# Hybrid attention, scan and MLP block on one core: a ring for keys and values, and other margins in the order planner

## The chip, the cores and the metric

The kernel runs on one core of a Trainium2 chip. The metric is the device time of one execution in microseconds, as the median of several runs. The program text runs once on the host and writes a fixed list of instructions for each engine: TensorE (PE), VectorE (DVE), ScalarE (ACT), GpSimd (POOL) and SyncE (SP), which issues all DMAs. Each engine works through its own list in order and waits on semaphores.

## The reference

One layer over 2048 tokens of width 1024, all in float32 (shortened):

```
h = rmsnorm(x); q, k, v, z, xbc, dt, qx = split(h @ w_in)
q, k = partial_rope(rmsnorm per head)                      # 8 query heads, 2 key/value heads, 64 wide
attn_out = windowed_gqa(q, k, v, sink)                     # each 128-token block sees blocks j-1, j, j+1
ssd_out  = bidirectional_ssd(z, xbc, dt, ...)              # 16 heads, chunks of 128 tokens, both directions
xatt_out = memory_cross_attention(qx, mem, ...)            # 256 memory tokens
x = x + concatenate([attn_out, ssd_out, xatt_out]) @ w_out
x = x + square(relu(rmsnorm(x) @ w_mlp_up)) @ w_mlp_down   # hidden width 4096
```

In the windowed attention a query at position p sees keys with |p - p'| <= 128, so of block j-1 the upper triangle, of block j everything, of block j+1 the lower triangle; the softmax has one more column, the sink.

## The kernel before

A large product is made of two-part operands (hi + lo, rounded to the fp32r format) in three matmuls. There are three stages.

Stage 1 (`stage1`, line 1095) goes over the tokens in two halves, the second half first. For each it loads x transposed, splits it (`split`, line 466: ScalarE writes hi, another engine lo), and makes keys and values, the convolution columns, cross attention, and queries. `kvdt_tiles` (line 887) stores for each block of 128 tokens the transposed keys to `k_d` in DRAM (four rows of 128 tokens: hi and lo of two heads), laid out as 128 partitions x 4 x 2048 tokens, and the values to `v_d`.

Stage 2 (`stage2`, line 1331) goes over the 16 blocks j and the two key/value heads: 32 times an attention unit (`att_unit`, line 1201) and a scan unit (`ssd_unit`, line 1264), and 24 times a column block of the gate z (`z_col`, 24 full-width matmuls of 512 columns). `att_load` (line 1190) loads for each unit its queries, its window of two or three key blocks (tile `kw`, two buffers) and of value blocks (`vw`, two buffers). The unit makes the scores of four heads, adds a mask of three blocks (line 524: triangle, zeros, other triangle), takes exp, transposes, and multiplies with the values. This last product, and the scan's product per head, have stationary operands of 64 columns and write one half of the partitions; two of them run side by side.

Stage 3 (`stage3`, line 1618) makes the output projection for 8 pairs of token tiles (`out_pair`, line 1370; the weights w_out come through two raw buffers, `raw` in line 605, and `out_weights` splits them), then the MLP in a seven-product scheme (`seven`, line 1520), whose moving blocks come from `xc_d` and whose sums are added to rows of x1, loaded at the stage's start.

The order on all engines is written out by a planner. Every operation is first recorded with a cost and its dependences (`add`, line 197). `plan` (line 277) then runs a model of the engines: each time an engine is free it takes, of the operations whose inputs are ready, the one earliest in the program among those that are safe, otherwise the one that becomes safe first. Safe is ready plus a margin (`margin`, line 269), which depends on the engine of the producer o and of the consumer q. For a DMA the model counts 475 ns on SP, then

```
dma = max(dma, s + 1100) + o.bytes / 360.0
o.end = dma + 900
```

A switch between 64-column and full-width matmuls counts 95 ns. `schedule` (line 389) then issues the operations in the order of their planned starts, and the engines keep to it whatever the real times are.

SBUF is cut into regions with names (`memory1` to `memory4`), each reused by a later stage once everything that touched it is done; inside a region a tag has a number of buffers that are used in turn.

Of the kernel before, what the change touches and what calls it, by code (L numbers as in the profile page):

```python
# [10 lines left out]
F32 = mybir.dt.float32  # L11
F32R = mybir.dt.float32r
I32 = mybir.dt.int32
AF = mybir.ActivationFunctionType
# [5 lines left out]
P = 128  # L20
D = 1024
T = 2048
NJ = T // P
# [7 lines left out]
EPS = 1e-6  # L31
# [4 lines left out]
NCOL, NROW = sum(n for _, n in COLS), sum(n for _, n in ROWS)  # L36
# [37 lines left out]
class Program:  # L74
# [193 lines left out]
    @staticmethod  # L268
    def margin(o, q):

        if o.eng == "SP":
            return 2500
        if q.eng == "PE" and o.eng != "PE":
            return 800
        return 0 if o.eng == q.eng or o.eng == "PE" else 200

    def plan(self):

# [172 lines left out]
class Hybrid:  # L451
# [53 lines left out]
    def constants(self):  # L505
        nc, a = self.nc, self.a
        sizes = dict(ident=128, ones=128, eps=1, cols=NCOL, r1=16)
        self.mem.use("const", F32, **{"c_" + k: (n, 1) for k, n in sizes.items()})
        sizes = dict(triU=128, triL=128, amask=384, rows=NROW, dt=512, acs=512, wst=512, dec=512, edge=48, negA=32)
        self.mem.use("late", F32, **{"c_" + k: (n, 1) for k, n in sizes.items()})  # L510

        def c(name, shape):
            return self.mem.tile([P] + shape, F32, "c_" + name)

        self.ident = c("ident", [P])
        make_identity(nc, self.ident)
        self.ones = c("ones", [P])
        nc.gpsimd.memset(self.ones, 1.0)
        self.triU = c("triU", [P])
        self.triL = c("triL", [P])  # L520
        for t, sgn in ((self.triU, 1), (self.triL, -1)):
            nc.gpsimd.affine_select(out=t, in_=self.ones, compare_op=ALU.is_ge, fill=0.0, base=0,
                                    pattern=[[sgn, P]], channel_multiplier=-sgn)
        self.mask = c("amask", [3 * P])
        nc.gpsimd.memset(self.mask, 0.0)
        for o, sgn in ((0, 1), (2 * P, -1)):
            m = self.mask[:, o:o + P]
            nc.gpsimd.affine_select(out=m, in_=m, compare_op=ALU.is_ge, fill=NEG, base=0,
                                    pattern=[[sgn, P]], channel_multiplier=-sgn)
        self.eps = c("eps", [1])  # L530
        nc.gpsimd.memset(self.eps, EPS)

        cols, rows = c("cols", [NCOL]), c("rows", [NROW])
        first = NCOL - 256
        self.load(cols[:, :first], a["cols"][:, :first])

        def cut(t, table, name, shape=None):
            at = sum(n for k, n in table[:[k for k, _ in table].index(name)])
            v = t[:, at:at + dict(table)[name]]
            return v.rearrange("p (a b) -> p a b", a=shape[0]) if shape else v  # L540

        self.w_mix, self.w_mem, self.w_mlp, self.w_ssd, self.cb, self.sd = (
            cut(cols, COLS, n) for n in ("w_mix", "w_mem", "w_mlp", "w_ssd", "cb", "sd"))
        self.cw, self.cos, self.sin = cut(cols, COLS, "cw", (NXC,)), cut(cols, COLS, "cos", (NJ,)), cut(cols, COLS, "sin", (NJ,))
        for v in (cut(cols, COLS, "cw"), self.cb):
            nc.vector.tensor_scalar(v, v, 0.5, None, ALU.mult)
        self.qw, self.kw, self.xqw, self.xkw, self.sink, self.dtb, self.al = (
            cut(rows, ROWS, n) for n in ("qw", "kw", "xqw", "xkw", "sink", "dtb", "al"))
        self.r1 = c("r1", [NJ])
        self.dt = c("dt", [NJ, 32])  # L550
        self.acs = c("acs", [NJ, 32])
        self.wst = c("wst", [NJ, 32])
        self.dec = c("dec", [NJ, 32])
        self.edge = c("edge", [NXC, 4])
        self.negA = c("negA", [32])
        yield
        self.load(cols[:, first:], a["cols"][:, first:])
        self.load(rows, a["rows"].rearrange("(o n) -> o n", o=1).broadcast_to([P, NROW]))
        nc.vector.tensor_scalar(self.qw, self.qw, 0.125, None, ALU.mult)
        nc.vector.tensor_tensor(self.xkw, self.xkw, self.xqw, ALU.mult)  # L560
        nc.scalar.activation(self.negA, self.al, AF.Exp)
        nc.vector.tensor_scalar(self.negA, self.negA, -1.0, None, ALU.mult)
        yield
# [20 lines left out]
    def memory2(self):  # L584
        m = self.mem
        m.use("E", F32R, mv=(1024, 2), qs=(512, 2))
        m.use("A1", F32R, sr=(1024, 2), kw=(768, 2), vw=(192, 2, F32))
        m.use("A0", F32, fr=(1024, 2), xw=(512, 2), ao=(256, 2))
        m.use("B", F32, xs=(1280, 2), sf0=(512, 2), sf1=(512, 2), xb=(1536, 2))
        m.use("C", F32, ap=(1536, 2))  # L590
        m.use("X0", F32R, zxh=(512, 8))
        m.use("X1", F32R, zxl=(512, 8))
        m.use("X2", F32, apT=(1536, 2), y=(512, 2))
        m.use("X3", F32R, zwh=(1024, 2), zwl=(1024, 2))
        m.use("W0", F32, bk=(1024, 2), pb=(1024, 2))
        m.use("W1", F32, ee=(1024, 2), zth=(512, 2))
        m.use("Z", F32, zwr=(1024, 1), zraw=(512, 2), zrow=(512, 1), zt=(512, 2))

    def memory3(self):
        m = self.mem  # L600
        for i, (h, l) in enumerate((("X0", "X1"), ("late", "A1"), ("X2", "A0"), ("W0", "W1"))):
            m.use(h, F32R, **{f"woh{i}": (1024, 4)})
            m.use(l, F32R, **{f"wol{i}": (1024, 4)})
        m.use("X3", F32R, ah=(512, 4), al=(512, 4))
        m.use("Z", F32, raw=(1024, 2), ar=(512, 2))
        m.use("B", F32, row=(1024, 4), xn=(1024, 2), yr=(512, 4))
        m.use("C", F32, mb=(512, 6))
        m.use("E", F32R, ms=(1024, 2), zg=(512, 2))
# [17 lines left out]
    def scratch(self):  # L626
        dp = self.ctx.enter_context(self.tc.tile_pool(name="dram", bufs=1, space=DRAM))
        d = lambda name, shape, dt=F32: dp.tile(shape, dt, name=name, tag=name)
        self.r_d = d("r_d", [T])
        self.xbc_d = d("xbc_d", [NJ, P, NXC, P])  # L630
        self.xst_d = d("xst_d", [NJ, P, XST_W])
        self.v_d = d("v_d", [NJ, P, P])
        self.k_d = d("k_d", [P, 4, T])
        self.q_d = d("q_d", [NJ, P, 8 * P])
        self.row_d = d("row_d", [NJ, 2, 2, 2, 2, 8, 64])
        self.srow_d = d("srow_d", [NJ, 2, 2, 8, 3, P])
        self.erow_d = d("erow_d", [NJ, 2, 2, 8, P])
        self.pb_d = d("pb_d", [NJ, P, D])
        self.z_d = d("z_d", [NJ, P, 8, P])
        self.mix_d = d("mix_d", [NJ, P, 16, P])  # L640
        self.x1_d = d("x1_d", [T, D])
        self.xc_d = d("xc_d", [2, 8, 2, 4, P, BLK])
# [244 lines left out]
    def kvdt_tiles(self, pool, t0, tts, ps):  # L887

        nc = self.nc
# [7 lines left out]
        kk = pool.tile([P, BLK], F32, "tm")  # L897
        self.head_norm(pool, [ps[tt][:, 0:P] for tt in tts], 2, 64, r, self.kw, kk, "tm")
        for i in range(4):
            j = j0 + i  # L900
# [11 lines left out]
                nc.tensor.transpose(pt[:, n * P:(n + 1) * P], ktv[:, n, :], self.ident)  # L912
            ko = pool.tile([P, 4, P], F32R, "ko")
            nc.scalar.copy(ko, pt.rearrange("p (i t) -> p i t", i=4))
            self.store(self.k_d[:, :, j * P:(j + 1) * P], ko.bitcast(F32))

    def dt_half(self, pool, t0):

# [269 lines left out]
        self.store(self.z_d[b * 4:b * 4 + 4, :, c, :].rearrange("j p t -> p j t"), zt.rearrange("p (j t) -> p j t", j=4))  # L1188

    def att_load(self, pool, j, kv):  # L1190
        lo, hi = max(j - 1, 0), min(j + 1, NJ - 1)
        n = hi - lo + 1
        qs = pool.tile([P, 4, P], F32R, "qs")
        self.load(qs.bitcast(F32).rearrange("p h t -> p (h t)"), self.q_d[j][:, kv * BLK:(kv + 1) * BLK])
        kk = pool.tile([P, 2, 3 * P], F32R, "kw")
        self.load(kk[:, :, :n * P].bitcast(F32), self.k_d[:, kv * 2:kv * 2 + 2, lo * P:(hi + 1) * P])
        vv = pool.tile([P, 3, 64], F32, "vw")
        self.load(vv[:, :n, :], self.v_d[lo:hi + 1, :, kv * 64:kv * 64 + 64].rearrange("j t c -> t j c"))
        return n, lo - j + 1, qs, kk, vv

    def att_unit(self, pool, j, kv):
        nc = self.nc
        n, m0, qs, kk, vv = self.att_load(pool, j, kv)
        w = n * P
# [6 lines left out]
        mask = self.mask[:, m0 * P:m0 * P + w]  # L1211
        for i in range(4):
            ps = self.ps()[:, :w]
            nc.tensor.matmul(ps, qs[:, i, :], kk[:, 0, :w], start=True, stop=False)
            nc.tensor.matmul(ps, qs[:, i, :], kk[:, 1, :w], start=False, stop=True)
            nc.vector.tensor_tensor_reduce(pr[:, i, :], ps, mask, 1.0, NEG, ALU.add, ALU.max, mx[:, i:i + 1])
        nc.vector.tensor_tensor(mx, mx, sk, ALU.max)
        nc.vector.tensor_scalar(ng, mx, -1.0, None, ALU.mult)
# [112 lines left out]
    def stage2(self):  # L1331
# [4 lines left out]
        for n, (ts, ring) in enumerate(((self.mv, "fr"), (self.sr, "fr"))):  # L1336
            raw = pool.tile([P, 1024], F32, ring)
            self.load(raw, self.a["pick"][n])
            for t in ts:
                nc.scalar.copy(t, raw)  # L1340
        self.sf = []
        for g in range(2):
            st = pool.tile([P, BLK], F32, f"sf{g}")
# [387 lines left out]
```

## Time and profile before

| | us |
|---|---|
| median of 3 runs | 2802.86 (2800.09 to 2805.92) |
| the profiled execution | 2797.64 |
| its span, first to last instruction | 2795.8 |
| PE busy | 2743.8 (98%) |
| DVE, ACT, POOL busy | 1887.1, 1361.1, 554.1 |
| share of the DMA queue in 16 engines' span | 55.5% |

PE, the matrix engine, is busy nearly all the time. Busy time of PE includes the time of matmuls in the pipeline, so idle time alone doesn't show everything. The granted clock of PE is given as a share of full speed (1.00 is 2.4 GHz).

### The profile page before, as it was taken

To read this page: it belongs to the slowest core of one execution; us is meant where nothing else is said; L and a number is where in the kernel's file an instruction comes from. 1 tells how busy PE (TensorE), PEld (TensorE's weight loads), DVE (VectorE), ACT (ScalarE), POOL (GpSimd) and SP (SyncE) were. 2 spreads that over 40 slices of the span, in tenths; PEclk is the share of its full clock that TensorE was granted. 3 is DMA by queue.
4 is the path that set the end of the run, shared out by engine and by line. 5 is a ranking of instruction groups with operands and counts; after the bars stand their busy time and mean duration, and the time that the engine had idled before them with its cause. 6 is when DMAs were issued, how large, how long until landed. Compare 5 with 4: busy or idle time off the path is not lost.

```text
span 2795.8 us, 37466 instructions
## 1 busy us (share of the span) xinstructions
PE 2743.8 (98%) x13628; PEld 2253.9 (81%) x13628; DVE 1887.1 (67%) x3133; ACT 1361.1 (49%) x2294; POOL 554.1 (20%) x488
## 2 busy tenths in 40 slices
PE   8999999999999999999999999999999999999999
PEld 8878887788777777778888788888888888888887
DVE  5884568856666686666666776675758485757666
ACT  5645543354567676843333453535344353535352
POOL 3303444445344454411010000000000000000000
PEclk9999999999999999999999999999999999999999
DMA  6661345544878787765555862627173744536251
GB/s 217 188 205 54 117 142 178 184 143 171 280 248 254 227 270 237 212 226 201 188 196 188 329 231 95 226 69 253 55 234 128 269 145 136 181 99 210 90 166 61
DMA packets 286429, 510.29 MB, mean 183 GB/s; under 512 B 36386, under 2 KB 125090, under 8 KB 286244
## 3 DMA queue, kind: packets, MB, share of 16 engines
q1 hardware_dynamic: 286244, 507.89, 55.5%
q8 instruction: 108, 1.77, 0.3%
q14 instruction: 77, 0.63, 0.1%
HBM read 390.36 MB, written 117.45 MB: 182 GB/s over the span
## 4 chain that ended last, share of the span: by engine, by line
PE 76%; DMA 4%; DVE 1%; ACT 1%; issue 1%; POOL 1%; SPq 0%; DVEq 0%; POOLq 0%; ACTq 0%
PE bank L404 76%; DMA Z<-in_xT_dram 1%; DMA W<-erow_d 1%; DMA Z<-mix_d 0%; DMA X<-xc_d 0%; ACT C L404 0%; DMA E<-z_d 0%; DMA A<-k_d 0%; DMA xst_d<-B 0%; ACT X L404 0%; DMA B<-mix_d 0%; DMA B<-x_d 0%; DVE X L404 0%; DVE Z L404 0%; DMA Z<-in_w_z_dram 0%
## 5 line engine op out<-in xcount | busy, mean ns | idle before, releaser
L404 PE MATMUL bank<-X,late 128*128 128x512 f32 x1792 | 553.7, 390 | 5.4 <-DMA X<-xc_d 5.4
L404 PE MATMUL bank<-A,E 128*128 128x512 f32 (+2 forms) x1152 | 405.2, 380 | 0.0
L404 PEld LDWEIGHTS bank<-X,late 128*128 128x128 f32 x1792 | 336.9, 188 | 75.8 <-issue 5.8
L404 PE MATMUL bank<-X,A 128*128 128x512 f32 (+1 forms) x1264 | 397.0, 390 | 0.0
L404 PE MATMUL bank<-W,X 128*128 128x512 f32 (+1 forms) x1536 | 341.5, 374 | 9.1 <-ACT W L404 7.3
L404 PE MATMUL bank<-late,E 128*128 128x512 f32 x896 | 348.5, 389 | 0.0
L404 PE MATMUL bank<-late,C 128*128 128x512 f32 x896 | 348.5, 389 | 0.0
L404 PE MATMUL bank<-X,X 128*128 128x512 f32 x1216 | 327.3, 406 | 3.0 <-ACT X L404 2.3
L404 PE MATMUL bank<-X,W 128*128 128x512 f32 x1344 | 325.1, 397 | 3.4 <-ACT W L404 3.4
L404 PEld LDWEIGHTS bank<-W,X 128*128 128x128 f32 x1536 | 268.0, 191 | 54.0 <-ACT W L404 7.3
L404 PEld LDWEIGHTS bank<-X,W 128*128 128x128 f32 x1344 | 249.1, 189 | 56.2 <-ACT W L404 3.6
L404 PEld LDWEIGHTS bank<-X,X 128*128 128x128 f32 x1216 | 225.7, 189 | 60.3 <-issue 10.6
L404 PEld LDWEIGHTS bank<-A,E 128*128 128x128 f32 x1152 | 211.6, 188 | 44.4 <-issue 6.4
L404 PEld LDWEIGHTS bank<-X,A 128*128 128x128 f32 (+1 forms) x1264 | 192.3, 173 | 51.5 <-ACT X L404 5.3
L404 DVE TENSOR_TENSOR A<-Z,late 128x1024 fp32r<-128x1024 f32 x100 | 122.1, 1222 | 138.5 <-ACT late L404 136.6
L404 DVE TENSOR_TENSOR B<-B,bank 128x512 f32<-128x512 f32 x286 | 189.7, 682 | 31.6 <-PE bank L404 31.3
L404 PEld LDWEIGHTS bank<-late,C 128*128 128x128 f32 x896 | 168.2, 188 | 35.0
L404 PEld LDWEIGHTS bank<-late,E 128*128 128x128 f32 x896 | 168.2, 188 | 34.9
L404 ACT CAST late<-Z 128x1024 fp32r<-128x1024 f32 x100 | 105.1, 1051 | 141.5 <-PE bank L404 102.1
L404 ACT ACTIVATE C<-C,small 128x384 f32<-128x384 f32 (+1 forms) x256 | 144.2, 602 | 51.9 <-DVE small L404 51.7
L404 ACT ACTIVATE W<-W 128x512 f32<-128x512 f32 x224 | 133.7, 627 | 61.5 <-DVE W L404 59.2
L404 ACT CAST E<-W 128x1024 fp32r<-128x1024 f32 x64 | 67.3, 1051 | 164.5 <-PE bank L404 164.5
(176 smaller groups left out, 4418.0 us busy)
## 6 DMA issues: line engine op xcount, KB each, us to landing
X<-xc_d SPq DMA_DIRECT2D x112, 1024.0 KB
xc_d<-E SPq DMA_DIRECT2D x56, 512.0 KB
Z<-in_w_z_dram SPq DMA_DIRECT2D x32, 512.0 KB
W<-erow_d SPq DMA_DIRECT2D x64, 256.0 KB
X<-in_w_up_dram SPq DMA_DIRECT2D x32, 512.0 KB
A<-in_w_up_dram SPq DMA_DIRECT2D x32, 512.0 KB
X<-in_w_down_dram SPq DMA_DIRECT2D x32, 512.0 KB
A<-in_w_down_dram SPq DMA_DIRECT2D x32, 512.0 KB
```

What stands on the lines that cost most here:

```text
L404: o.fn(*[fix(x) for x in o.args], **{k: fix(x) for k, x in o.kw.items()})
```

## The change

All edits go together. (1) `margin`: a 64-column matmul (`q.half`) is safe 9000 ns after its inputs are ready, a DMA that waits for compute 6000 ns (before 200, and 0 behind PE), a matmul behind another engine 1200 (800), other pairs of engines 400 (200). A consumer of a DMA keeps 2500. (2) The keys are stored block by block, and each block of keys and values, for both heads, is loaded once, at the first unit of a chunk, into place b mod 3 of a ring of three; the mask tile has six blocks, and each unit reads three (or two) of them from an offset that fits the ring's turn. (3) `eps`, which nothing reads, is set on VectorE and copied in place by ScalarE as the first instructions, instead of on GpSimd. (4) `raw` of stage 3 has three buffers.

```diff
@@ margin
         if o.eng == "SP":
             return 2500
+        if q.eng == "PE" and q.half:
+            return 9000
+        if q.eng == "SP":
+            return 6000
         if q.eng == "PE" and o.eng != "PE":
-            return 800
-        return 0 if o.eng == q.eng or o.eng == "PE" else 200
+            return 1200
+        return 0 if o.eng == q.eng or o.eng == "PE" else 400
@@ constants
+        self.eps = c("eps", [1])
+        nc.vector.memset(self.eps, EPS)
+        nc.scalar.activation(self.eps, self.eps, AF.Copy)
         self.ident = c("ident", [P])
...
-        self.mask = c("amask", [3 * P])
+        self.mask = c("amask", [6 * P])
         nc.gpsimd.memset(self.mask, 0.0)
-        for o, sgn in ((0, 1), (2 * P, -1)):
-            m = self.mask[:, o:o + P]
+        for o, sgn in ((0, 1), (2, -1), (3, 1), (5, 1)):
+            m = self.mask[:, o * P:(o + 1) * P]
...
-        self.eps = c("eps", [1])
-        nc.gpsimd.memset(self.eps, EPS)
@@ memory2, memory3, scratch, kvdt_tiles
-        m.use("A1", F32R, sr=(1024, 2), kw=(768, 2), vw=(192, 2, F32))
+        m.use("A1", F32R, sr=(1024, 2), kr=(1536, 1), vr=(384, 1, F32))
-        m.use("Z", F32, raw=(1024, 2), ar=(512, 2))
+        m.use("Z", F32, raw=(1024, 3), ar=(512, 2))
-        self.k_d = d("k_d", [P, 4, T])
+        self.k_d = d("k_d", [NJ, P, 4, P])
-            self.store(self.k_d[:, :, j * P:(j + 1) * P], ko.bitcast(F32))
+            self.store(self.k_d[j], ko.bitcast(F32))
@@ att_load
-        lo, hi = max(j - 1, 0), min(j + 1, NJ - 1)
-        n = hi - lo + 1
+        if kv == 0:
+            for b in range(j and j + 1, j + 2):
+                self.load(self.kr[:, b % 3].bitcast(F32), self.k_d[min(b, NJ - 1)])
+                self.load(self.vr[:, b % 3], self.v_d[min(b, NJ - 1)])
         qs = pool.tile([P, 4, P], F32R, "qs")
         self.load(qs.bitcast(F32).rearrange("p h t -> p (h t)"), self.q_d[j][:, kv * BLK:(kv + 1) * BLK])
-        kk = pool.tile([P, 2, 3 * P], F32R, "kw")
-        self.load(kk[:, :, :n * P].bitcast(F32), self.k_d[:, kv * 2:kv * 2 + 2, lo * P:(hi + 1) * P])
-        vv = pool.tile([P, 3, 64], F32, "vw")
-        self.load(vv[:, :n, :], self.v_d[lo:hi + 1, :, kv * 64:kv * 64 + 64].rearrange("j t c -> t j c"))
-        return n, lo - j + 1, qs, kk, vv
+        at, n = (1, 2) if j == NJ - 1 else (0, 3 if j else 2)
+        role = 4 if j == NJ - 1 else (1, 0, 2)[j % 3]
+        k = lambda l: self.kr[:, at:at + n, kv * 2 + l, :]
+        return n, role, qs, (k(0), k(1)), self.vr[:, at:at + n, kv * 64:kv * 64 + 64]
```

In `att_unit` the score matmuls read `kk[0]` and `kk[1]` instead of `kk[:, 0, :w]` and `kk[:, 1, :w]`, and `stage2` makes the two ring tiles `kr` and `vr` once.

## Rows read from the trace of the kernel before

**Rows 1.** The page: busy time of the engines, share of the span, instructions
```profile
PE 2743.8 (98%) x13628; PEld 2253.9 (81%) x13628; DVE 1887.1 (67%) x3133; ACT 1361.1 (49%) x2294; POOL 554.1 (20%) x488
```

**Rows 2.** Busy time by stage: window, PE, PEld, DVE, ACT, POOL (instructions), PEclk, DMA, GB/s
```profile
0.00:750.00 750.00, 727.47 (x3838) 609.38 (x3838) 508.43 (x1010) 370.01 (x673) 292.45 (x254) 0.99 0.52 167
750.00:1190.00 440.00, 426.52 (x2700) 328.64 (x2702) 306.75 (x760) 313.44 (x726) 209.68 (x169) 0.98 0.80 245
1190.00:1230.00 40.00, 33.22 (x146) 25.29 (x141) 24.78 (x40) 15.78 (x21) 11.06 (x13) 0.91 0.76 258
...
1585.00:1625.00 40.00, 34.57 (x146) 28.18 (x145) 18.52 (x22) 17.65 (x26) 0.00 (x0) 0.91 1.02 381
1625.00:2795.80 1170.80, 1166.97 (x5149) 965.96 (x5147) 787.41 (x821) 515.62 (x655) 0.00 (x0) 1.00 0.46 152
```

**Rows 3.** PE's timeline where it idled longest: start, us, what, [idle before <- what ended it]
```profile
353.32 1.22 PE L404 MATMUL bank<-X,W 128*128 128x512 f32 x2 [3.37 <-ACT W L404]
...
753.31 0.48 PE L404 MATMUL bank<-const,C 128*128 128x128 f32 x1 [4.42 <-ACT C L404]
...
1205.32 0.79 PE L404 MATMUL bank<-const,E 128*128 128x1 f32 x4 [2.18 <-POOL E L404]
...
1217.73 0.38 PE L404 MATMUL bank<-const,E 128*128 128x1 f32 x2 [1.40 <-POOL E L404]
...
1604.20 1.19 PE L404 MATMUL bank<-X,late 128*128 128x512 f32 x2 [5.43 <-DMA X<-xc_d]
```

**Rows 4.** Busy time by stage again, two short stretches after the last of these stops
```profile
1604.20:1607.54 3.34, 3.34 (x8) 2.69 (x9) 0.00 (x0) 0.00 (x0) 0.00 (x0) 0.50 1.05 408
1607.60:1610.94 3.34, 3.34 (x16) 2.71 (x16) 0.00 (x0) 0.00 (x0) 0.00 (x0) 1.00 1.05 415
```

**Rows 5.** Timeline of the first 8 us, ScalarE and PE
```profile
4.94 1.28 ACT L404 ACT_TABLE_LOAD   x1 [4.94 <-DMA B<-in_xT_dram]
6.23 0.72 ACT L404 ACTIVATE X<-B,const 128x512 fp32r<-128x512 f32 x1
...
7.33 0.61 PE L404 MATMUL bank<-W,X 128*128 128x288 f32 x1 [7.33 <-ACT W L404]
```

**Rows 6.** PE's timeline around 64-column matmuls (128*64): the first, one, and the last stretch
```profile
739.93 1.09 PE L404 MATMUL bank<-A,B 128*64 128x128 f32 x16
...
922.71 2.46 PE L404 MATMUL bank<-X,X 128*128 128x512 f32 x10
925.10 1.09 PE L404 MATMUL bank<-A,B 128*64 128x128 f32 x16
...
1190.50 1.04 PE L404 MATMUL bank<-A,B 128*64 128x128 f32 x16
```

**Rows 7.** PE's timeline, two short stops in stage 1
```profile
114.57 0.44 PE L404 MATMUL bank<-const,B 128*128 128x128 f32 x2 [0.70 <-ACT B L404]
...
528.03 1.55 PE L404 MATMUL bank<-B,E 128*128 128x512 f32 x3 [0.44 <-POOL B L404]
```

**Rows 8.** SP's timeline at the border to the MLP: DMA issues, count
```profile
1575.11 0.37 SPq L404 DMA_DIRECT2D X<-xc_d  x1
...
1583.96 3.37 SPq L404 DMA_DIRECT2D B<-x_d  x6
...
1588.06 1.26 SPq L404 DMA_DIRECT2D B<-x_d  x2
...
1591.39 6.85 SPq L404 DMA_DIRECT2D X<-xc_d  x3
```

**Rows 9.** DMA issues of key and value blocks: count, KB each
```profile
A<-k_d SPq DMA_DIRECT2D x28, 384.0 KB
...
A<-v_d SPq DMA_DIRECT2D x28, 96.0 KB
```

**Rows 10.** The chain of waits in stage 2: start, us, two DMA pieces
```profile
738.54 8.66 DMA A<-k_d
...
786.65 3.83 DMA Z<-in_xT_dram
```

More of the change, by code (lines that the diff above doesn't have):

```diff
@@ L508, in constants @@
         self.mem.use("const", F32, **{"c_" + k: (n, 1) for k, n in sizes.items()})
-        sizes = dict(triU=128, triL=128, amask=384, rows=NROW, dt=512, acs=512, wst=512, dec=512, edge=48, negA=32)
+        sizes = dict(triU=128, triL=128, amask=768, rows=NROW, dt=512, acs=512, wst=512, dec=512, edge=48, negA=32)
         self.mem.use("late", F32, **{"c_" + k: (n, 1) for k, n in sizes.items()})
@@ L1213, in att_unit @@
             ps = self.ps()[:, :w]
-            nc.tensor.matmul(ps, qs[:, i, :], kk[:, 0, :w], start=True, stop=False)
-            nc.tensor.matmul(ps, qs[:, i, :], kk[:, 1, :w], start=False, stop=True)
+            nc.tensor.matmul(ps, qs[:, i, :], kk[0], start=True, stop=False)
+            nc.tensor.matmul(ps, qs[:, i, :], kk[1], start=False, stop=True)
             nc.vector.tensor_tensor_reduce(pr[:, i, :], ps, mask, 1.0, NEG, ALU.add, ALU.max, mx[:, i:i + 1])
@@ L1340, in stage2 @@
                 nc.scalar.copy(t, raw)
+        self.kr = pool.tile([P, 3, 4, P], F32R, "kr")
+        self.vr = pool.tile([P, 3, P], F32, "vr")
         self.sf = []
```

## The prediction

> **What bounds the kernel now.** I read the page first. TensorE (PE) is busy for 2743.8 of 2795.8 us and its weight loads for 2253.9 [rows 1], so time can leave only where PE idles, runs at the lower clock, or loses time between two matmuls. Then busy time by stage [rows 2]: the MLP from 1625 us on has 5149 matmuls in 1166.97 us, 0.2266 us each, and DMA at 0.46; nothing in the change touches these matmuls. Idle PE time is 750 - 727.47 = 22.5 us in the first stage (7.33 of it before the first matmul [rows 5]), 13.5 in the second, 6.8 in 1190 to 1230, 5.4 in 1585 to 1625. Then PE's timeline, where the idle time stands [rows 3]: 3.37 us where the second half of the tokens begins, 4.42 at the start of stage 2, 2.18 and 1.40 in the first output pair, 5.43 in the first MLP block. Each long stop is also followed by a stretch at the lower clock: right after the 5.43, 8 matmuls fit into 3.34 us at granted 0.50, and 16 into the next 3.34 us at 1.00 [rows 4]; 0.50 is 1.2 GHz, 1.00 is 2.4. The 0.91 of the two 40 us stretches [rows 2] is 40 x 0.09 = 3.6 us lost each. So at most some 48 us of idle and, by the rounded clocks of rows 2 (7.5 + 8.8 + 3.6 + 3.6), 23 us of low clock are open to any change, 2.5% of the span.
>
> The profiled execution took 2797.64 us (span 2795.8 and 1.8 around it); the median of the three runs is 2802.86, 5.2 more. I sum against 2797.64 and carry the difference over to the median.
>
> **Start.** Before, ScalarE's first instruction is a table load of 1.28 us that begins when the first x block lands at 4.94; the split after it starts at 6.23 and the first matmul at 7.33 [rows 5]. The new memset and one-column copy need no DMA, so the load ends by about 3 us and the first split can start at 4.94. PE is busy almost without a break afterwards, so the shift is carried through: -1.3; bounds 0 (the weight block lands no earlier) and -1.3. The two added mask selections and the wider memset lie on GpSimd after the identity; nobody waits for them before stage 2: 0.
> By the Trainium skill (ScalarE: Activation LUTs, section What ACT_TABLE_LOAD costs) a table switch costs about 2.66 us, since a drain of some 1.38 us goes with the load. The trace disagrees: the activation starts 0.01 us after the load's end [rows 5]. By the page the sum would be 1.4 us lower.
>
> **64-column matmuls gathered.** Ten full-width matmuls ahead of a 64-column stretch take 925.10 - 922.71 = 2.39 us instead of 10 x 0.2266 = 2.27 [rows 6]: 0.12 us for one change of width, and I take the way back as like it. From 739.93 to 1191.5 PE's timeline has 110 such changes, so 55 stretches, for 32 attention units and 32 scan units [rows 6] (the first and the last stretch of 55). A 64-column matmul now counts as safe only 9 us after it is ready, against a unit period of 440 / 32 = 13.8 us, so one stretch can hold a unit's attention output and its scan output. 32 stretches would leave 64 changes: 46 x 0.12 = -5.5. I take -3.5, as not every pair will meet. The other bound is +3: while such a matmul stands back although it has long been ready, PE may take a younger instruction and stop for it.
>
> **Wider margins for PE (800 to 1200 ns) and between the other engines (200 to 400).** They change no instruction, only the order that the planner writes out. PE works in order, so what it waits for today is a producer that came more than 0.8 us later than planned. Eight stops of 0.44 to 1.06 us between 113 and 528 us sum to 5.9 us [rows 7] (the first and the last of 8); 0.4 us more margin takes up to 8 x 0.4 = 3.2 from them, and stage 2's scattered waits have the same cause. I take -4. Bounds: all idle time of both stages but the start, and but the 4.42 that I price below: -(22.5 - 7.3 + 13.5 - 4.4) = -24; and +6, if the new order only puts eight such stops elsewhere and adds none of the gain.
>
> **Third buffer for w_out's raw blocks.** It lets one more block load while two are split. In 1190 to 1230 [rows 2] the gaps end on GpSimd's gate sums [rows 3], which it doesn't touch: -1; bounds 0 and the whole 6.8 + 3.6 = -10.4.
>
> **DMA queue: stores and loads that depend on compute stand back 6 us.** SP takes what has been safe the longest in program order only among the safe ones, otherwise what becomes safe first; 6 us for all makes it nearly first come, first served. Where it shows: at the border to the MLP six and then two loads of x1 (512 KB each, 4 MB) leave at 1583.96 and 1588, ahead of X<-xc_d at 1591.39 in program order [rows 8], though the x1 rows are needed much later; at the 381 GB/s of that stretch [rows 2] 4 MB are 11 us, and PE stops 5.43 us for xc_d [rows 3]. The block before it left at 1575.11 [rows 8], as soon as a half product had read its buffer; the next half product takes 24 x 0.2266 = 5.4 us, so the next buffer was free at about 1580.5, before the x1 rows' places were. Served in order of coming, the first of these loads passes the x1 loads; the second does not. I take -5 of the 5.43 + 3.4 of low clock; bounds -8.8, and +6, if the second block stops PE as the first did.
>
> **Ring of three key and value blocks.** Before, a unit loads its own window: 28 loads of 384 KB and 28 of 96 KB, and four short ones of 256 and 64 KB each [rows 9]; after, 17 of 256 and 17 of 64 KB: 14.7 MB become 5.4, in a stage whose DMA share is 0.80 [rows 2]. PE instructions are the same: masks are read at another offset, the width stays. DMA load is on no engine's path but where PE waits for it, at the start of stage 2 (4.42 us, behind loads that took 8.66 us [rows 10]): -2. But the ring also adds a wait. A block j+1 takes the place of j-2, so its load is issued after the last scores of the chunk before, and the next scores need it; before, each unit had a second buffer and a whole unit's time of lead. The planner counts 0.73 us of transfer and 2.0 of latency, and 2.5 of margin, 5.2 us from issue to use. Loads in this stage land 3.83 us (256 KB) to 8.66 us (384 KB) after issue [rows 10], so 0 to 3.5 us late, 14 times (three of the 17 find an empty place). Queued behind the waiting score matmuls is everything on PE. I take +3, near the 3.83, since PE has gate matmuls to put in between. Together +1; bounds -8.5 (the 4.42, its low clock, and 0.7) and 14 x 3.5 - 2 = +47. The 16 stores of key blocks write the same bytes in runs of 512 elements instead of 128, in a stage with DMA at 0.52 [rows 2]: 0.
> By the Trainium skill (DMA: Bandwidth & Descriptors, section Anatomy of one DMA) a load costs some 2.0 us plus its bytes at 436 GB/s, measured there on GpSimd's path; a 256 KB block would be an estimated 2.6 us, within the margin, and the ring's wait would cost nothing: sum 3 lower. The rows at 8.66 speak against it while the DMA engines are loaded.
>
> **Sum.** -1.3 - 3.5 - 4 - 1 - 5 + 1 = -13.8: 2783.8 for an execution like the profiled one, 2789 as a median. Its own range is 8 us to each side, 2781 to 2797.
>
> **Rivals.**
> All stops at the stage borders go (4.42, 2.18, 1.40, 5.43 and their low clock, about 13.4 + 12), with the small terms: some -32, 2770. For it: all of them are stops behind a DMA order or a buffer. Against: two wait for GpSimd.
> Nothing in the end: start and gathering bring -4.8, the new order moves the other stops instead of removing them, and the ring costs 3: -1.8, 2801. For it: each stop is an accident of one order, and the new order has its own accidents.
> The ring comes late (slower). Place: the first score matmul after each of 14 reloads. Price: 14 x the mean lateness. My sum holds 0.21 us each; from (13.8 + 3) / 14 = 1.2 us each the gain is gone, and at 2.5 us each it is +35 instead of +3: -13.8 + 32 = +18.2, 2821. For it: 8.66 us, and DMA share 0.80; against it: 3.83 us, and the 9 MB that leave this stage.
>
> **How the numbers follow.** About 0.2%, 5.6 us, is what a measurement of this kernel can tell from no change. Forecast 0.47 (0.44 of it faster by more than that), borders all gone 0.10, nothing 0.20 (0.17 within, 0.03 slower), late ring 0.23 (0.20 slower, 0.03 within). So faster 0.54, within 0.23, slower 0.23. The range 2768 to 2815 takes in the good rival and half of the late ring; what is left out is under 2 in 10.
>
> **What would show it.** First matmul near 6.0 us. Fewer than 80 changes of width in stage 2. DMA share of stage 2 near 0.72. The stop of 5.43 us under 2 us, with a higher granted clock from 1585 to 1625. Stops of PE before score matmuls that end on the key blocks' loads would show the late ring. Wrong I'd be if the MLP's 0.2266 us per matmul moved, or if new stops of over 1 us stood in stage 1 or 2 where none were.

## The result, and the profile after

The changed kernel takes 2783.84 us (median of 4 runs, 2779.78 to 2786.43) beside 2802.47 for the kernel before (4 runs, 2800.09 to 2805.92): ratio 0.9933, 95% interval 0.992 to 0.9947, that is 18.6 us shorter. The profiled execution took 2783.82, with a span of 2781.4.

The page of the changed kernel, the line that answers to [rows 1]: busy time, share of the span and instructions of each engine.

```profile
PE 2730.2 (98%) x13628; PEld 2256.1 (81%) x13628; DVE 1894.8 (68%) x3134; ACT 1362.7 (49%) x2295; POOL 564.8 (20%) x489
```

The same matmuls, with 13.6 us less busy PE. Busy time by stage of the changed kernel, as [rows 2]: window, PE, PEld, DVE, ACT, POOL, PEclk, DMA share, GB/s.

```profile
0.00:750.00 750.00, 727.07 (x3838) 608.15 (x3839) 513.24 (x1020) 377.65 (x695) 294.66 (x252) 0.99 0.53 168
750.00:1190.00 440.00, 423.15 (x2748) 338.39 (x2747) 313.45 (x759) 310.67 (x709) 217.66 (x173) 0.99 0.73 225
1190.00:1230.00 40.00, 35.26 (x149) 28.70 (x148) 28.58 (x44) 17.11 (x23) 10.78 (x12) 0.91 0.70 244
...
1585.00:1625.00 40.00, 37.04 (x157) 30.20 (x156) 22.14 (x26) 21.47 (x32) 0.00 (x0) 0.96 1.03 391
1625.00:2781.40 1156.40, 1152.67 (x5086) 954.12 (x5084) 777.31 (x809) 505.07 (x641) 0.00 (x0) 1.00 0.45 150
```

The MLP keeps its pace: 1152.67 / 5086 = 0.2266 us per matmul, as before. Stage 2's DMA share fell from 0.80 to 0.73, and the border's clock rose from 0.91 to 0.96. Everything was gained ahead of the MLP. The longest stops of PE in the changed kernel, as [rows 3] (start, us, what, [idle before <- what ended it]):

```profile
341.41 1.02 PE L408 MATMUL bank<-X,W 128*128 128x512 f32 x2 [2.23 <-ACT W L408]
...
741.37 1.67 PE L408 MATMUL bank<-const,C 128*128 128x128 f32 x4 [4.70 <-ACT C L408]
...
1059.54 0.55 PE L408 MATMUL bank<-const,C 128*128 128x128 f32 x3 [2.31 <-ACT C L408]
...
1142.18 3.79 PE L408 MATMUL bank<-const,C 128*128 128x128 f32 x12 [3.93 <-ACT C L408]
...
1203.81 2.07 PE L408 MATMUL bank<-X,X 128*128 128x512 f32 x4 [4.62 <-ACT X L408]
...
1589.88 0.70 PE L408 MATMUL bank<-X,late 128*128 128x512 f32 x2 [2.96 <-DMA X<-xc_d]
```

The two stops for GpSimd's sums are gone, and the 5.43 is 2.96. But stage 2 has stops of 3.93 and 2.31 us in new places, and 4.62 stands in the first output pair. Stage 2 wasn't without such stops before: two stood there that [rows 3] leaves out, 1.44 us at 881.41 and this one:

```profile
1150.67 1.99 PE L404 MATMUL bank<-const,C 128*128 128x128 f32 x4 [2.57 <-ACT C L404]
```

The two traces alone don't tell which edit moved which stop.

### The profile page after: what moved, and what is told of

The parts are those of the page before. It is cut to its first block, busy times and chain, and to the rows that moved or that the text cites. A ratio compares the mean times of both kernels' runs of the same rounds, so it can differ in the third digit from the quotient of the medians.

```text
span 2781.4 us, 37411 instructions
## 1 busy us (share of the span) xinstructions
PE 2730.2 (98%) x13628; PEld 2256.1 (81%) x13628; DVE 1894.8 (68%) x3134; ACT 1362.7 (49%) x2295; POOL 564.8 (20%) x489
## 2 busy tenths in 40 slices
DMA packets 264187, 500.77 MB, mean 180 GB/s; under 512 B 24130, under 2 KB 98626, under 8 KB 264004
## 4 chain that ended last, share of the span: by engine, by line
PE 87%; DMA 6%; DVE 3%; ACT 2%; issue 1%; SPq 0%; POOL 0%; ACTq 0%; DVEq 0%; POOLq 0%
PE bank L408 87%; DVE B L408 1%; DMA W<-erow_d 1%; DMA Z<-in_w_out_dram 1%; DMA z_d<-Z 1%; DMA xst_d<-B 1%; ACT C L408 0%; DVE X L408 0%; DMA Z<-in_xT_dram 0%; DMA X<-xc_d 0%; SPq L408 0%; ACT B L408 0%; DMA xbc_d<-B 0%; DMA B<-in_xT_dram 0%; DVE A L408 0%
## 5 line engine op out<-in xcount | busy, mean ns | idle before, releaser
L408 PE MATMUL bank<-X,X 128*128 128x512 f32 x1216 | 318.4, 402 | 7.9 <-ACT X L408 5.5
```

What stands on the lines that cost most here:

```text
L408: o.fn(*[fix(x) for x in o.args], **{k: fix(x) for k, x in o.kw.items()})
```

## The experiments

Each edit makes the planner write a new order for the whole kernel, so what an edit does itself has to be told from what any new order does. All runs were compared with the kernel before on the same chip.

**The edits one by one on the kernel before.** First the margins of PE and between the other engines alone:

```diff
-            return 800
-        return 0 if o.eng == q.eng or o.eng == "PE" else 200
+            return 1200
+        return 0 if o.eng == q.eng or o.eng == "PE" else 400
```

> The kernel before with the two compute margins alone (800 to 1200 ns ahead of PE, 200 to 400 between the other engines). Theory from the two traces: most of the 8.8 us that the two halves of stage 1 lost besides the start are due to these margins, so 6 to 10 us less than before. My step in the prediction: 4 us less. Rival, an accident of each written order: anything within 5 us of before, on either side, and stops of PE in stage 1 as many as before.

Measured: 2798.06 us, ratio 0.9993 (0.9983 to 1.0003). Nothing on the whole.

SyncE's margin alone (`if q.eng == "SP": return 6000`):

> The kernel before with the 6 us margin of DMAs alone. Theory: it acts at the border to the MLP, where the xc_d loads leave sooner, and hardly anywhere else: 2 to 5 us less, with the 5.43 us stop at about 3. Rival: stage 1's loads are what gets better under it, then 6 to 10 us less, and the margins of the compute engines do little. Second rival, an accident of each order: within 5 us of before on either side.

Measured: 2805.24, ratio 1.0017 (1.0009 to 1.0026), slower, although the stop at the MLP's border shrank as in the changed kernel. The loss stands in the second half of stage 1 (398.8 us for 391.8 before) and in stage 2 (470.5 for 458.7). PE's timeline at the border in this run:

```profile
1616.26 0.70 PE L406 MATMUL bank<-X,late 128*128 128x512 f32 x2 [2.58 <-DMA X<-xc_d]
```

The 64-column margin alone (`if q.eng == "PE" and q.half: return 9000`):

> The kernel before with the 9 us margin of 64-column matmuls alone. Theory: the changes of width in stage 2 fall from 110 to about 62 at 0.1 us each, 48 x 0.1 = 5 us less; time to the first score unchanged. Rival: standing back holds up the attention outputs, PE stops elsewhere in stage 2, and the 5 us are given back: within 2 us of before.

Measured: 2807.00, ratio 1.0023 (1.0013 to 1.0033), slower, although the changes of width in stage 2 fell from 110 to 58. The saving that was forecast did come: from the first score to the last 64-column matmul PE is busy for 437.7 us (2842 matmuls) where it was 444.1 (2846): 6.4 us for 52 changes of width, 0.12 us each, as the prediction had it. But it idles there for 25.2 us where it was 15.0, and the stretch as a whole is longer. So the rival holds in kind, though the time is past its 2 us.

The ring alone, with its masks and the blockwise layout of the keys, as in the change's diff:

> The kernel before with the ring, its masks and the key layout alone. Theory: the DMA share of stage 2 falls from 0.80 to about 0.73 and PE gains little from it, as no PE instruction waits for a key block: between 2 us less and 3 us more. Rival, the late ring: score matmuls wait for key blocks, 5 us more or worse. Rival, relief: the loads of z's inputs and of erow land sooner, 5 us less or better.

Measured: 2820.92, ratio 1.0072 (1.006 to 1.0084), 20 us slower. The late ring would show PE waiting for `A<-k_d`. What PE waited for from 750 to 1190 us of this run (engine and line, what it waited for, us in total, times, longest), the three largest:

```profile
PE bank L404 <- ACT X L404: 8.5, 10, 1.9
PE bank L404 <- ACT A L404: 5.7, 7, 2.1
PE bank L404 <- ACT C L404: 3.4, 10, 1.6
```

No wait ends on a key block. Stage 2 takes 473.8 us for 458.7, and 10.3 of these 15 us are idle time of PE (25.3 for 15.0), in many short waits for ScalarE and VectorE; no stop is over 2.2 us. The ring's own wait is there, but on SP: its key loads waited for PE 34.1 us in all, 13 times, up to 8.9 us, where the kernel before has no such wait. No stop of PE comes of that: of its 37 waits from 735 to 1190 us none leads, along the chain of releases 15 us back, to a key load. The late-ring rival is refuted here in its place, though not in its sign.

**What a new order costs by itself.** The kernel before with 780 and 820 ns in place of its 800 ns for PE, a step that has nothing to bring:

> A control: the kernel before with the margin ahead of PE at 780 instead of 800 ns, too little to mean anything by itself, but the planner writes out another order. If an order's own accidents are small, the time is within 0.2% of before (5.6 us). If they are what the single edits showed (minus 2 to plus 20 us), it lies 5 us or more away, on either side.

> The same control on the other side, 820 instead of 800 ns. Small accidents: within 5.6 us of before. Large ones: 5 us or more away, not the same way as 780 has to go.

Measured: 2803.60, ratio 1.0014 (1.0004 to 1.0024), and 2804.12, ratio 1.0015 (1.0006 to 1.0024). And the changed kernel with 1180 and 1220 in place of 1200:

> The control on the changed kernel: 1180 instead of 1200 ns. If the gain of 18.6 us is the edits' own, this is within 5.6 us of the changed kernel, some 2784 us. If the changed kernel is a lucky order, this is slower than it, 2790 to 2805 us.

> The control on the changed kernel on the other side: 1220 instead of 1200 ns. The edits' own gain: some 2784 us, within 5.6. A lucky order: 2790 to 2805 us.

Measured: 2788.87, ratio 0.9965 (0.9954 to 0.9976), and 2781.22, ratio 0.9938 (0.9918 to 0.9958). So an arbitrary new order is worth some 4 us either way (the two neighbours of the changed kernel are 7.7 us apart), and the order of before is a lucky one, 4 us better than its two neighbours. The losses of the SyncE margin and of the gathering alone are about this large; the ring's 20 us are beyond it. The changed kernel's gain is beyond it too: it and its two neighbours lie 11 to 19 us under before.

**The third raw buffer alone** on the kernel before:

```diff
-        m.use("Z", F32, raw=(1024, 2), ar=(512, 2))
+        m.use("Z", F32, raw=(1024, 3), ar=(512, 2))
```

> The kernel before with one thing changed: three raw buffers for the blocks of w_out for two. Theory A (the third buffer is what shortens the output projection by some 4.5 us in every run of the changed kernel, where none of the other single edits shortened it): first to last matmul of the output projection's gate near 343 to 344 us for 347 to 351, the time 3 to 5 us shorter, 2794 to 2797. Rival (the stops of the first output pair wait for GpSimd's sums and not for the weights, so the buffer gives nothing alone): 347 to 351 us there, 2799 to 2802.

Measured: 2791.63 (10 runs), ratio 0.9967 (0.9957 to 0.9978), 8.2 us shorter, and 343.7 us from the first to the last gate sum (the one-column matmuls that end GpSimd's sums): theory A holds in its stretch, with more gain in the time than it asked for. In this run the 40 us from 1190 on, the third of [rows 2]:

```profile
1190.00:1230.00 40.00, 39.81 (x181) 31.70 (x180) 29.37 (x44) 17.70 (x25) 12.19 (x13) 1.00 0.77 276
```

181 matmuls for 146, at clock 1.00 for 0.91: 35 x 0.2266 = 7.9 us, about the whole gain. What ended PE's waits there (columns as above), before:

```profile
PE bank L404 <- POOL E L404: 3.6, 2, 2.2
PE bank L404 <- DVE A L404: 1.8, 2, 1.4
PE bank L404 <- ACT late L404: 0.9, 1, 0.9
```

and with three buffers:

```profile
PE bank L404 <- DVE A L404: 0.2, 1, 0.2
```

So not only GpSimd's sums held PE: 2.7 of these 6.3 us ended on the splits of weight blocks (ScalarE's write of the high part into `late`, VectorE's write of the low part into `A`). SP's timeline (start, us from first issue to last, what, count) shows where the loads for the sums stood. Before:

```profile
1188.39 0.33 SPq L404 DMA_DIRECT2D Z<-in_w_out_dram  x1
1191.12 0.32 SPq L404 DMA_DIRECT2D mix_d<-A  x1
1192.03 0.33 SPq L404 DMA_DIRECT2D Z<-in_w_out_dram  x1
1193.10 0.81 SPq L404 DMA_DIRECT2D B<-in_x_dram  x2
1193.96 0.91 SPq L404 DMA_DIRECT2D B<-mix_d  x2
...
1205.73 0.80 SPq L404 DMA_DIRECT2D E<-z_d  x2
1208.26 6.26 SPq L404 DMA_DIRECT2D Z<-in_w_out_dram  x2
```

With three buffers:

```profile
1189.26 0.32 SPq L404 DMA_DIRECT2D mix_d<-A  x1
1190.44 0.81 SPq L404 DMA_DIRECT2D B<-in_x_dram  x2
1191.30 0.90 SPq L404 DMA_DIRECT2D B<-mix_d  x2
...
1202.29 0.80 SPq L404 DMA_DIRECT2D E<-z_d  x2
1205.40 3.12 SPq L404 DMA_DIRECT2D Z<-in_w_out_dram  x3
```

With two buffers SP waits 3.3 us ahead of the weight load at 1188.39 and 0.5 us ahead of the one at 1192.03, each time until VectorE has read a raw buffer. With three no weight load stands there, and the row loads (B<-in_x, B<-mix_d) leave 2.7 us earlier. The chain of waits of before leads from such a row load to both sums:

```profile
1193.96 6.94 DMA B<-mix_d
...
1205.32 0.38 PE bank L404 x2
...
1206.15 6.13 DMA E<-z_d
...
1216.09 0.73 POOL E L404
...
1217.73 0.38 PE bank L404 x2
```

The pair of weight loads that takes SP 6.26 us, 5.5 of them a wait for a raw buffer, is not on this chain: the gate loads (E<-z_d) ahead of it are 3.4 us late already. With three buffers PE's own work is 73.9% of the chain from 1185 to 1235 us, for 42.1% before. But SP also waited 2.3 us ahead of 1191.12, for an attention output, and the order around it is a new one. How much of the 2.7 us is the buffer's and how much the order's is not shown.

**The changed kernel without the ring** (two places, old layout, old masks; all else as changed):

> The changed kernel without the ring of key and value blocks: two places again, each half's blocks loaded as in the kernel before, its two layouts of K and its masks; margins, gathering, the third raw buffer and the store margin stay as changed. Theory A (the ring costs scheduling slack in the second stage, as it did alone: +20 us on the whole and some +10 there): 2772 to 2779, stage 2 shorter than 460 us. Theory B (the wider margins and the gathering take the ring's cost away, and its fewer loads are worth something): 2784 to 2792. Theory C (the order's accidents outweigh the ring, some 4 us each way): 2780 to 2788, and nothing can be said.

Measured: 2784.89 (8 runs), ratio 0.9955 (0.994 to 0.9969), stage 2 468.6 us. The changed kernel has 0.9933 (0.992 to 0.9947): the intervals overlap, so the ring brings nothing that can be told, and it doesn't cost its 20 us here. Theory A fell; B and C are not told apart.

**The table load alone**, in the order of before:

```diff
+            t = self.pool.tile([P, 1], F32, name="first", tag="first")
+            self.tc.nc.vector.memset(t, EPS)
+            self.tc.nc.scalar.activation(t, t, AF.Copy)
```

> The kernel before in its own order of instructions, with one thing added: the activation table is loaded by a copy of the constant ahead of the first stage, as in the changed kernel. Theory A (the load of the table stood on the chain to the first matmul): first matmul near 6.0 us for 7.3, the time 1.3 us shorter, 2801. Rival (the transfers of x decide the first stage anyway): first matmul earlier, but no gain at the half's end, 2802 to 2803.

The timeline of this run's start:

```profile
0.80 1.28 ACT L404 ACT_TABLE_LOAD   x1 [0.80 <-PEq L1660]
...
4.97 0.72 ACT L407 ACTIVATE X<-B,const 128x512 fp32r<-128x512 f32 x1 [2.68 <-DMA B<-in_xT_dram]
...
6.06 3.25 PE L407 MATMUL bank<-W,X 128*128 128x288 f32 x12 [6.06 <-ACT W L407]
```

The first matmul starts 1.27 us earlier, as priced. The time: 2802.27 (11 runs) beside 2798.98 (18 runs), ratio 1.0010 (1.0001 to 1.0018). The rival's time came, but not in the place that it named: the lead is still there at the half's end (338.44 us for 340.76 at the second half's first matmul) and at the first scores (729.65 for 732.53). Stage 2 loses it, with 463.4 us for 458.7. Why it does so in the same order, and why this kernel came out 3 us longer, is open.

**The changed kernel with eight loads moved** on SyncE, and nothing else:

```diff
...
+        acc = [n for n in range(len(order)) if moves(n, "x1_d")][:8]
+        to = [n for n in range(acc[-1], len(order)) if moves(n, "xc_d")][2]
+        held = [order[n] for n in acc]
+        order = [o for n, o in enumerate(order[:to + 1]) if n not in acc] + held + order[to + 1:]
```

Here `moves(n, src)` is true where operation n of the written order is a DMA that reads `src`.

> The changed kernel in its own order, with one thing moved: on SyncE the eight loads of the last token block's x1, which leave ahead of the MLP's next three loads of xc in the changed kernel, leave behind these three. Theory A (the first matmuls of the MLP wait for xc behind these eight transfers): the stop of 2.96 us at the MLP's border goes to under 0.5, the time 3 to 4.7 us shorter, 2779 to 2781. Rival (xc waits for its own stores and not for the queue, or the x1 loads come too late for the last additions): the stop stays above 2 us, 2783 to 2786.

SP's timeline in the changed kernel, as [rows 8]:

```profile
1572.58 4.57 SPq L408 DMA_DIRECT2D B<-x_d  x8
1577.50 0.37 SPq L408 DMA_DIRECT2D X<-xc_d  x1
...
1579.96 1.03 SPq L408 DMA_DIRECT2D X<-xc_d  x1
...
1584.51 1.16 SPq L408 DMA_DIRECT2D X<-xc_d  x1
```

and in this run, with its one remaining stop of PE and its 40 us at the border:

```profile
1572.59 0.36 SPq L414 DMA_DIRECT2D X<-xc_d  x1
...
1573.95 0.36 SPq L414 DMA_DIRECT2D X<-xc_d  x1
...
1579.16 0.36 SPq L414 DMA_DIRECT2D X<-xc_d  x1
1579.58 7.17 SPq L414 DMA_DIRECT2D B<-x_d  x8
```

```profile
1601.52 0.73 PE L414 MATMUL bank<-X,late 128*128 128x512 f32 x2 [0.62 <-DMA X<-xc_d]
```

```profile
1585.00:1625.00 40.00, 39.38 (x174) 32.26 (x173) 27.47 (x31) 25.47 (x39) 0.00 (x0) 1.00 1.04 412
```

The stop shrinks from 2.96 to 0.62 us, the clock goes from 0.96 to 1.00, and 174 matmuls stand where 157 did: 17 x 0.2266 = 3.9 us, inside theory A's 3 to 4.7, though the stop is not quite under its 0.5. The time is 2776.13 (5 runs), ratio 0.9924 (0.9911 to 0.9937), the shortest median of all and shorter than theory A's 2779; its interval overlaps that of the changed kernel, so as a whole time the step beyond it is not told apart.

**The stages side by side.** Lengths between marks on PE's timeline, from one profiled execution of each of the 14 kernels, sorted by whether they hold the edit that should act there (mean, and lowest to highest; which edit in brackets):

```
stretch                                              without               with            mean diff
start to the first matmul            [table load]     7.6 (7.1-8.1)     6.2 (5.8-6.7)      -1.4
first half of stage 1                [1200/400]     332.7 (328.6-336.2) 331.1 (328.4-335.2) -1.6
second half of stage 1               [1200/400]     393.7 (391.2-398.8) 387.8 (385.6-389.7) -5.9
stage 2, scores to last 64 columns   [gathering]    465.0 (458.7-473.8) 462.0 (455.0-468.6) -3.0
from there to the last gate sum      [raw x 3]      361.3 (355.5-364.5) 354.9 (350.7-358.9) -6.4
first MLP stretch, to bank<-late,E   [SP 6000]       85.6 (85.1-86.6)    82.2 (80.9-83.3)   -3.4
rest of the MLP                                    1142.2              1142.2               0.0
```

The halves of stage 1 begin with a first 128x288 matmul, and the MLP's first stretch with the first bank<-X,late. The MLP row leaves out the kernel with the moved loads (79.0). Five of the kernels counted as "with" are the changed one and its four variants, which hold the other edits too; what an edit does alone is seen in one kernel each. Three rows have ranges that don't touch: the start, the second half of stage 1 and the MLP's first stretch. In the row of the raw buffers the overlap comes from the kernel with 780 ns; from the first gate sum to the last alone it is 341.6 to 345.1 against 347.3 to 350.7. In stage 2 the spread is larger than the difference. It is made of two parts that go against each other: with the gathering PE is busy for 439.5 us in the mean for 446.8 without, and idle for 22.8 for 18.5. How much of that is no order at all: the kernel with moved loads has the changed kernel's order up to the border, and its stage 2 took 455.0 us where that took 462.1.

## Why the prediction was right, step by step

The time and its sign were right: 2789 forecast, 2783.84 measured. The gain was 18.6 us for a sum of 13.8. But the terms in it were not all, and that errors of several us on either side left the sum this near is in part luck: 20 ns of one margin alone move the changed kernel 5 us (2788.87).

**Third raw buffer: -1 forecast, -8.2 measured alone**, the largest error and the largest term. It failed in two readings. It said that the gaps from 1190 to 1230 end on GpSimd's sums, but 2.7 us of them end on the splits of weight blocks. And it read the name behind "<-" as the cause: the sums were late since the row loads they need left SP late, in a list in which weight loads that waited for their buffer stood ahead. What the buffer itself did to these row loads is not shown apart from the new order. The bound of 10.4 held. With the other edits one stop of 4.62 us is back there (1203.81), behind a weight load of 7.66 us. As a whole time 8.2 us is hardly more than the 7.7 between the changed kernel's two neighbours, so the stretch is the safer measure: it is 6.4 us shorter on average, and from the first gate sum to the last, where the ranges don't touch, 5.6.

**PE and engine margins: -4 forecast.** Seen as -5.9 in the second half of stage 1, in the mean of the six kernels that have them; the one that has nothing else took 388.4 us there, for 391.2 to 398.8 in those without. Alone they gave nothing on the whole: of the 3.4 us that this half was shorter than before, the first half took back 1.8 (335.2 us for 333.4) and stage 2 another 2.2 (460.9 for 458.7).

**SyncE's margin: -5 forecast, -3.4 at the border.** The first xc block did not pass the x1 loads, as the prediction had it: all eight leave ahead of it. But they leave in one run, and the xc block follows 1577.50 - 1572.58 = 4.9 us after their first, where it was 1591.39 - 1583.96 = 7.4 us [rows 8]; the 2.5 us between are the 5.43 - 2.96 that the stop lost. What the step had in mind is what the moved loads then did: 0.62 us and clock 1.00. The forecast of under 2 us for this stop was wrong.

**Start: -1.3 forecast; -1.4 at the first matmul, nothing in the time** of the run that does only this. The step failed where it said that the shift is carried through: it was, up to stage 2, and was lost there.

**Gathering: -3.5 forecast; the saving came and was taken back.** The 62 changes of width are under the 80 named, and 48 x 0.12 = 5.8 us of drained matmuls should be gone. They are: in stage 2 the changed kernel's PE is busy for 437.6 us where it was 444.1, with as many matmuls (2848 for 2846), and the kernel with the gathering alone for 437.7. But PE's idle time there, summed over all gaps of the trace, is 24.7 us for 15.0, and 25.2 with the gathering alone. That a matmul which stands back lets something younger stop PE was the +3 bound, and the length of stage 2 with the gathering alone, 462.6 us for 458.7, is near it. In the mean of all kernels the idle time is 4.2 us more with the gathering; but the same order up to the border gave 24.7 in the changed kernel and 18.7 in the one with the moved loads, so how much of it is the gathering's is not told.

**Ring: +1 forecast; +20 alone, nothing that can be told with the other edits.** Key loads are 17 of 256 KB for 28 of 384 and 4 of 256 [rows 9], and no PE wait ends on one in any of the five kernels that have the ring. The wait that the prediction priced stands on SP instead (34.1 us alone, 21.0 in the changed kernel), and no stop of PE was found behind it. Alone the ring cost 20 us, most of it by many short waits for ScalarE and VectorE. Why it makes so poor an order alone is open: the margins between the engines (200 against 400 ns) may be the rescue, but no run separates them.

**The test for being wrong.** New stops of over 1 us in stage 2 (2.31, 3.93) did come, as did the sum, though the 2.57 and the 1.44 of before were overlooked. The prediction had named them as what would refute it; what falls with them is that its terms can be added: the SyncE margin, the gathering, the ring and the other margins, each run alone, sum to 4.8 + 6.6 + 20 - 2 = +29 us, the buffer gives -8, the table load +3, and all together -19. The rivals "nothing" (2801) and "late ring" (2821) are out, and "borders all gone" (2770) too, with 4.70, 4.62 and 2.96 us of stops still at the borders.

The stop at stage 2's start stayed (4.42, now 4.70), the chain in front of it now being a store and a weight load:

```profile
726.31 7.71 DMA z_d<-Z
...
734.10 5.75 DMA Z<-in_w_z_dram
...
740.81 2.19 ACT C L408 x6
```

## What to carry to other kernels

The engine named at a stop is the last to come, not the cause: follow the chain back to the queue, ask which waiting instruction at its head holds the loads behind it, and check that this instruction is on the chain. Where a planner writes the order, measure first what a step that means nothing does (here 20 ns of a margin: 4 us, 40 ns: 7.7), and judge an edit by the stretch it acts on, in several orders, not by the total of one. Look at busy and idle time of a stretch apart: a saving in one can be real and lost in the other. An extra buffer for weights was worth more here than 9.5 MB of traffic saved (510.29 to 500.77 MB).

## What was not expected of the hardware

Stops of one length at one place can leave the clock at either level. After the 2.96 us there were 10 matmuls at granted 0.66 in 3.34 us and then 14 at 0.84, where the 5.43 us of before gave 8 and then 16 [rows 4]:

```profile
1589.88:1593.22 3.34, 3.34 (x10) 2.68 (x11) 0.69 (x1) 0.62 (x1) 0.00 (x0) 0.66 1.06 410
1593.30:1596.64 3.34, 3.34 (x14) 2.65 (x14) 0.00 (x0) 0.00 (x0) 0.00 (x0) 0.84 1.05 410
```

The 0.66 and the 0.84 are means over both levels: from 1591.0 to 1594.3 the granted clock was 0.50 (1.2 GHz), before and after it 1.00 (2.4 GHz). That is 6 + 2 = 8 matmuls lost after either stop. But in the changed kernel without the ring the same stop for xc_d was 2.88 us long, and the clock stayed at 1.00, with 164 matmuls in the 40 us at the border:

```profile
1585.00:1625.00 40.00, 37.12 (x164) 30.47 (x163) 22.62 (x26) 22.14 (x34) 0.00 (x0) 1.00 1.04 399
```

It stayed at 1.00 too after the 2.58 us of the kernel with SyncE's margin alone, and after the 0.62 us of the kernel with the moved loads. So a stop's length alone doesn't tell here what it costs, and the low clock behind a stop shouldn't be priced as certain. And one order gave stage 2 lengths 7 us apart (462.1 and 455.0), more than most of the edits are worth.
